# Borders between the stages of a two-layer decoder trunk rebuilt: order of the rows, of the expansion's products and of the contraction's sums

## The chip, the cores and the metric

The kernel runs on one core of a Trainium2 chip. The metric is device time in microseconds (us), the median of several executions. The engines are PE (matrix products), DVE (vector operations), ACT (activations, copies, casts), POOL (GpSimd) and SP, which here only issues DMAs. Each engine works through its own list of instructions in order; semaphores tie the lists together.

## What is computed

Two decoder layers over 1024 tokens of 1024 features, all in float32. Per layer, with gains left out:

```python
h = h + rmsnorm(mixer(rmsnorm(h)))        # layer 0: attention, layer 1: RG-LRU
u = rmsnorm(h)
f = square(relu(u @ w_up)) @ w_down       # 1024 -> 4096 -> 1024
h = h + rmsnorm(f)
h = h + rmsnorm(p @ w_proj) * sigmoid(h @ w_gate)
```

## The kernel before

**Precision.** Each float32 operand is split into a high and a low part (`split`: a cast on ACT, L115, and a subtraction on DVE, L116; names end in h and l), and each product runs as three matmuls, `mm3` (L147 to L149: high x high, high x low, low x high).

**The MLP** is done by Strassen's scheme in Winograd's form: seven products of half-size blocks in place of eight. Their operands are A11, A12, A22 (blocks of the weights) and S1 to S4 (sums of such blocks) on one side and B11, B21, B22, T1 to T4 (blocks and sums of the input, split once and kept in `comb`) on the other. "First half" and "second half" are the two halves of the tokens.

**The stages of a layer.** (1) The mixer. (2) `mix_out`: the output projection, row block by row block (eight of 128 tokens). Per row: 24 matmuls of 512 columns, a sum with the partial result `pt` (L954, two of 512 columns), a root mean square (square and sum on ACT L165, scale and power on POOL L167 and L170), a scaling with the gain on DVE (L174), the residual add on POOL (L888), the store of the row to `hD`, a second norm of the same kind, eight 128x128 transposes (L916) and the combinations of the blocks on DVE (`combine`, L934 to L941). Rows of the second half need those of the first (`held`), and the rows go in pairs, 4, 5, 0, 1, 6, 7, 2, 3 in layer 0. (3) `mlp_up`, the expansion: eight quads of 512 hidden features, each with seven products of 24 matmuls into pairs of PSUM banks, their sums, relu and square, and seven tiles of 512 KB that SP stores to DRAM (`hid`): already the block sums that the contraction needs. The order of the products is A11, A12, S2, S3, S1, A22, S4, with quads 0 and 1 starting together. (4) `mlp_down`, the contraction: four chunks of two quads, seven products of 48 matmuls, in the order A22, S1, S3, A11, S2, A12, S4. Each step loads two hidden tiles (`hraw`), splits them, and adds its result to its own accumulator (X and M tiles). In the last chunk 14 closing adds on DVE join the accumulators (L1109). (5) The gate: eight rows normed (`post`, once more with L888 on POOL), transposed (L183), multiplied with `ple_w_gate`.

**What sets the order.** The program is written stage by stage; a scheduler then fixes each engine's list before the run. `bufs` says how many buffers a name has, and a tile can't be written before the last reader of its buffer is done. `wAh` and `wAl`, the split weights, have three buffers each.

## Time and profile before

| | us |
|---|---|
| median of 3 runs | 2719.72 (2712.79 to 2722.66) |
| the profiled execution | 2716.89 |
| its span | 2715.1 |
| PE busy | 2515.9 (93%), mean granted clock 0.961 |
| DVE busy | 1685.8 (62%) |
| ACT busy | 1224.6 (45%) |
| POOL busy | 327.7 (12%) |

The stages of layer 0 end at about 652 (attention), 742 (output rows, norms and the first matmuls of the expansion), 1057.7 (expansion), 1378 (contraction), 1409 us (its norms); those of layer 1 lie 1212 us later. A view by stretch gives, for each engine, the busy time and the number of instructions in it, and the clock that was granted to PE. PE busy includes matmuls at a low clock, which take longer.

### The profile page before, as it was taken

How to read it: one execution, taken by the hardware profiler on the slowest of the kernel's cores; microseconds unless marked ns; L12 is line 12 of the kernel's file. 1: busy time of each engine (PE TensorE's matmuls, PEld its weight loads, DVE VectorE, ACT ScalarE, POOL GpSimd, SP SyncE). 2: the span in 40 equal slices, each digit the busy share in tenths (PEclk: the TensorE clock that was granted, in tenths of full speed). 3: DMA queues.
4: the chain of work that ended last, by engine and by line, in shares of the span. 5: the costliest groups of instructions: out<-in, count | busy, mean ns of one | idle time of the engine just before them, and what ended most of it. 6: DMA issues, size and time to landing. Idle time of an engine off the chain costs nothing. (4 is left out here: it accounts for less than half of the span.)

```text
span 2715.1 us, 31386 instructions
## 1 busy us (share of the span) xinstructions
PE 2515.9 (93%) x11681; PEld 2063.2 (76%) x11681; DVE 1685.8 (62%) x2094; ACT 1224.6 (45%) x1779; POOL 327.7 (12%) x398
## 2 busy tenths in 40 slices
PE   8899999988599999999969999998699999999969
PEld 7687888776478887877758788877578887877757
DVE  5565665765756656577774555654755665677862
ACT  4454555654434444433332366563443445433331
POOL 1312223313300000000050000002300000000050
PEclk9899999999799999999979999999799999999989
DMA  5747553435334447444353322245344446444253
GB/s 158 199 139 189 157 147 104 137 120 187 132 132 155 148 141 255 155 152 137 107 192 118 132 90 62 74 151 194 109 142 153 155 147 237 150 155 148 93 194 101
DMA packets 220893, 396.95 MB, mean 146 GB/s; under 512 B 16691, under 2 KB 118172, under 8 KB 220740
## 3 DMA queue, kind: packets, MB, share of 16 engines
q1 hardware_dynamic: 220740, 394.95, 44.9%
q8 instruction: 92, 1.51, 0.2%
q14 instruction: 61, 0.50, 0.1%
HBM read 273.63 MB, written 121.26 MB: 145 GB/s over the span
## 5 line engine op out<-in xcount | busy, mean ns | idle before, releaser
L148 PE MATMUL sc<-wAl,hh 128*128 128x512 f32 x896 | 356.2, 398 | 11.8 <-DVE wAl L116 11.8
L149 PE MATMUL sc<-wAh,hl 128*128 128x512 f32 x896 | 351.5, 393 | 0.0
L147 PE MATMUL sc<-wAh,hh 128*128 128x512 f32 x896 | 333.6, 396 | 12.9 <-ACT hh L115 12.9
L167 POOL TENSOR_SCALAR ms<-ss 128x1 f32<-128x1 f32 x112 | 49.5, 442 | 1877.2 <-ACT r L165 1598.4
L115 ACT CAST hh<-hraw 128x1024 fp32r<-128x1024 f32 x112 | 117.4, 1048 | 300.4 <-PE sc L148 294.5
L115 ACT CAST wAh<-S 128x1024 fp32r<-128x1024 f32 x128 | 134.2, 1048 | 198.1 <-PE sc L148 170.6
L148 PEld LDWEIGHTS sc<-wAl,hh 128*128 128x128 f32 x896 | 169.2, 189 | 59.6 <-DVE wAl L116 22.6
L116 DVE TENSOR_TENSOR hl<-hraw,hh 128x1024 fp32r<-128x1024 f32 x112 | 136.5, 1221 | 123.8 <-ACT hh L115 123.8
L147 PE MATMUL sc<-uh,wAh 128*128 128x512 f32 x512 | 201.9, 398 | 10.0 <-ACT wAh L115 10.0
L147 PEld LDWEIGHTS sc<-wAh,hh 128*128 128x128 f32 x896 | 169.2, 189 | 52.6 <-ACT hh L115 13.7
L149 PE MATMUL sc<-uh,wAl 128*128 128x512 f32 x512 | 205.9, 402 | 1.6 <-DVE wAl L116 1.6
L148 PE MATMUL sc<-ul,wAh 128*128 128x512 f32 x512 | 204.9, 400 | 0.0
L149 PEld LDWEIGHTS sc<-wAh,hl 128*128 128x128 f32 x896 | 168.7, 188 | 37.9
L116 DVE TENSOR_TENSOR wAl<-wraw,wAh 128x1024 fp32r<-128x1024 f32 (+1 forms) x100 | 129.7, 1298 | 71.9 <-ACT wAh L115 71.6
L116 DVE TENSOR_TENSOR wAl<-S,wAh 128x1024 fp32r<-128x1024 f32 x128 | 155.8, 1217 | 27.6 <-ACT wAh L115 27.6
L115 ACT CAST wAh<-wraw 128x1024 fp32r<-128x1024 f32 (+1 forms) x100 | 104.7, 1047 | 134.2 <-PE sc L148 53.6
L147 PE MATMUL sc<-xh,wAh 128*128 128x512 f32 x384 | 150.5, 392 | 1.8 <-ACT wAh L115 1.8
L149 PE MATMUL sc<-xh,wAl 128*128 128x512 f32 x384 | 152.1, 397 | 0.0
L148 PE MATMUL sc<-xl,wAh 128*128 128x512 f32 x384 | 151.9, 396 | 0.0
L402 DVE CUSTOM_DVE_ANT_0 sn<-sc,bias 128x128 f32<-128x128 f32 (+7 forms) x128 | 94.4, 754 | 67.0 <-PE tp L419 31.4
L147 PE MATMUL mm<-uh,wAh 128*128 128x512 f32 x312 | 127.7, 409 | 7.6 <-ACT st L342 6.6
L149 PE MATMUL mm<-uh,wAl 128*128 128x512 f32 x312 | 126.3, 405 | 0.0
(394 smaller groups left out, 6087.3 us busy)
## 6 DMA issues: line engine op xcount, KB each, us to landing
hraw<-hid SPq DMA_DIRECT2D x112, 512.0 KB
hid<-t SPq DMA_DIRECT2D x48, 512.0 KB
wq<-in_mlp_w_up_dram SPq DMA_DIRECT2D x44, 512.0 KB
wq<-in_mlp_w_down_dram SPq DMA_DIRECT2D x42, 512.0 KB
hD<-row SPq DMA_DIRECT2D x32, 512.0 KB
hid<-row SPq DMA_DIRECT2D x32, 512.0 KB
hid<-c SPq DMA_DIRECT2D x32, 512.0 KB
row<-hD SPq DMA_DIRECT2D x24, 512.0 KB
```

The lines of the kernel that those rows point to most:

```text
L115: nc.scalar.copy(out=dst_h, in_=src)
L116: nc.vector.tensor_tensor(out=dst_l, in0=src, in1=f32(dst_h), op=ALU.subtract)
L147: nc.tensor.matmul(dst, lh, rh, start=start, stop=False, skip_group_check=onto)
L148: nc.tensor.matmul(dst, lh, rl, start=False, stop=False, skip_group_check=onto)
L149: nc.tensor.matmul(dst, ll, rh, start=False, stop=stop, skip_group_check=onto)
L167: nc.gpsimd.tensor_scalar(out=ms, in0=ss, scalar1=1.0 / n, scalar2=eps, op0=ALU.mult, op1=ALU.add)
L402: nc.vector.tensor_tensor_reduce(out=sn[:, :w], in0=sps[:, :w], in1=bias, scale=-1.0, scalar=BIG, op0=ALU.add, op1=ALU.min, accum_out=nm)
```

## The change

- `mix_out`: the rows of the first half come first, 4, 5, 6, 7, 0, 1, 2, 3 in layer 0 and 0 to 7 in layer 1, and the attention's last units follow that order. A row's 24 matmuls go to one pair of banks with one load of the partial result. The norm's bias is added on ACT (`rms_row`), only the power stays on POOL, and the residual add is a fused scaling on DVE. The first half's transposed blocks are stored to DRAM (`uD`) and loaded again for the second half. Six products of the expansion, A11 and A12 of quads 0 to 2, are set among the rows by a list (`plan`); their weights use `wC` tiles and the usual buffers.
- `mlp_up`: the products come as A11, A12, S2, S1, S3, A22, S4. In the quads that were not begun early A11, S2, S3, A22 add up in one pair of banks, copied out in between, and S1, S4 in another. The hidden tiles of quads 0 and 1 are split on the spot (through `t`, three buffers) and stored as high and low tiles by POOL's queue (`hidS`).
- `first_step`: the contraction's first hidden tiles and weights are loaded and split before the expansion's last results.
- `mlp_down`: the order is A11, A12, S2, S3, A22, S1, S4, summed in PSUM; the 14 closing adds are gone. The first half of the rows is complete behind A22, two products before the end. The chunk of quads 0 and 1 comes last and loads its split tiles by POOL's queue, without splitting.
- The gate's norms use `rms_row` and DVE too; its products are as before.

Matmuls and transposes are the same in number. DVE's list goes from 2082 to 2057 rows, ACT's from 1541 to 1629, POOL's from 403 to 427, SP's from 985 to 951.

```diff
...
+    FACTOR = {"A11": B11, "A12": B21, "S2": T2, "S1": T1, "S3": T3, "A22": T4, "S4": B22}
+    NLEAD = 3
...
+    def rms_row(small, junk, src):
+
+        ss = small.tile([P, 1], F32, name="ss", bufs=4)
+        nc.scalar.activation(out=junk, in_=src, func=AF.Square, scale=1.0 / 32.0, accum_out=ss)
+        ms = small.tile([P, 1], F32, name="ms", bufs=4)
+        nc.scalar.activation(out=ms, in_=ss, func=AF.Identity, bias=eps1)
+        rs = small.tile([P, 1], F32, name="rs", bufs=4)
+        nc.gpsimd.tensor_tensor(out=rs, in0=ms, in1=nhalf, op=ALU.pow)
+        return rs
...
-            scale_gain(a, a, rs, g)
-            nc.gpsimd.tensor_tensor(out=h, in0=h, in1=a, op=ALU.add)
+            rs = rms_row(small, junk, a)
+            vec(ag, a, g, ALU.mult)
+            nc.vector.scalar_tensor_tensor(out=h, in0=ag, scalar=rs, in1=h, op0=ALU.mult, op1=ALU.add)
             return h
...
+                plan = [(out_row, 0), (out_row, 1), (combine, 0), (out_row, 2), (combine, 1), (out_row, 3),
+                        (combine, 2), (out_row, 4), (combine, 3), (out_row, 5), None, (combine, 4),
+                        (out_row, 6), None, (combine, 5), (out_row, 7), None, (combine, 6), None, None, None,
+                        (combine, 7)]
+                for step in plan:
+                    if step is None:
+                        leads.pop(0)()
+                    else:
+                        step[0](order[step[1]])
                 del wslots[3:]
...
+            def first():
+                a = st["A"] = pair_bank()
+                self.up_product(a, direct("A11", 0), "A11", True, True)
+                self.lead[q] = m1 = self.c.take()
+                nc.scalar.copy(out=m1[1], in_=a)
+
+            def second():
+                self.up_product(st["A"], direct("A12", 1), "A12", False, True)
+                c11 = row_tile()
+                self.squared(c11, st["A"])
+                nc.sync.dma_start(out=self.hidD[B11][q], in_=c11)
...
                     def keep(i, t):
-                        nc.sync.dma_start(out=hidD[i][q], in_=t)
...
+                        if q >= 2:
+                            nc.sync.dma_start(out=self.hidD[i][q], in_=t)
+                            return
+                        h, l = (hp.tile([P, D], F32R, name="t", bufs=3) for _ in range(2))
+                        split(h, l, t)
+                        for d, s in zip(self.hidS[i, q], (h, l)):
+                            nc.gpsimd.dma_start(out=d, in_=s)
...
+                    product(b, "S2", led)
+                    u2n, u2 = self.c.take()
+                    u3 = row_tile()
+                    if led:
+                        vec(u2, b, m1, ALU.add)
+                    else:
+                        nc.scalar.copy(out=u2, in_=b)
+                    c = pair_bank()
+                    product(c, "S1", True)
+                    product(b, "S3", False)
+                    if led:
+                        vec(u3, b, m1, ALU.add)
+                    else:
+                        nc.scalar.copy(out=u3, in_=b)
+                    vec(u3, c, u3, ALU.add)
...
+                    product(b, "A22", False)
...
+                    product(c, "S4", False)
+                    vec(u2, c, u2, ALU.add)
+                    c12 = u2
+                    self.squared(c12)
+                    if q == quads - 1:
+                        self.first_step()
...
+                if (i, q) in self.hidS:
+                    for d, s in zip((hh, hl_), self.hidS[i, q]):
+                        nc.gpsimd.dma_start(out=d, in_=s)
...
+        def first_step(self):
+            self.begin(0)
+            h, l = (t.rearrange("p (n a) c -> p n (a c)", n=2) for t in self.comb[B11])
+            self.ops0 = self.step("A11", [(h[:, n, :], l[:, n, :]) for n in range(2)])
...
-                        if c == last and name == "S4":
-                            for jj in range(2):
-                                h = home(jj)
-                                add(m6[jj], m6[jj], m1[jj])
...
+                for jj, b in product("A11", 0, True):
+                    onto((0, 0), jj, b, True)
+                for jj, b in product("A12", 1, True):
+                    onto((0, 0), jj, b)
+                for jj, b in product("S2", 0, False):
+                    temp("u2", jj, b)
+                for jj, b in product("S3", 0, False):
+                    temp("u3", jj, b)
+                for jj, b in product("A22", 0, False):
+                    onto((0, 1), jj, b, True)
+                yield c
+                for jj, b in product("S1", 2, True):
...
+                for jj, b in product("S4", 2, False):
...
-    m.mix_out(attn_w_out[0], (0, 2), lambda tb: x[0, tb * P:(tb + 1) * P, :], parts[0], (4, 5, 0, 1, 6, 7, 2, 3))
+    m.mix_out(attn_w_out[0], (0, 2), lambda tb: x[0, tb * P:(tb + 1) * P, :], parts[0], (4, 5, 6, 7, 0, 1, 2, 3))
```

**Where the lists change.** The names are tiles; `L116 ... wAl<-wq,wAh` (L118 in the new numbering) makes the low part of a weight, `S` are weight sums, `xl` and `ul` low parts of the combined input.

DVE in layer 0, from the last row's combination to the first products of the expansion, before:

```order
L116 TENSOR_TENSOR xl1_7482<-a_8091,xh1_7481 128x4x128
L116 TENSOR_TENSOR xl2_7484<-s_8028,xh2_7483 128x4x128
L116 TENSOR_TENSOR wAl_8179<-wq_8176,wAh_8178 128x1024
L116 TENSOR_TENSOR wAl_8211<-wq_8208,wAh_8210 128x1024
L116 TENSOR_TENSOR wAl_8246<-wraw_8243,wAh_8245 128x1024
L982 TENSOR_TENSOR S_8310<-wq_8311,wraw_8313 128x1024
L982 TENSOR_TENSOR S_8316<-S_8310,wq_8176 128x1024
L982 TENSOR_TENSOR S_8348<-wq_8176,wq_8311 128x1024
```

and after:

```order
L118 TENSOR_TENSOR ul01_130<-tp_8354,uh01_129 128x4x128
L118 TENSOR_TENSOR xl1_7572<-u_8362,xh1_7571 128x4x128
L118 TENSOR_TENSOR xl2_7574<-row_8359,xh2_7573 128x4x128
L878 TENSOR_TENSOR S_8390<-wq_8392,wq_8394 128x1024
L878 TENSOR_TENSOR S_8391<-S_8390,wraw_8397 128x1024
L878 TENSOR_TENSOR wraw_8397<-wraw_8397,wq_8392 128x1024
L878 TENSOR_TENSOR wq_8544<-wq_8544,S_8391 128x1024
L878 TENSOR_TENSOR S_8608<-wq_8610,wraw_8612 128x1024
L118 TENSOR_TENSOR wAl_8401<-S_8391,wAh_8400 128x1024
```

Before, the first three low weights stand right behind the last combination. Now five weight sums stand between it and the first low weight, that of S2.

ACT in the middle of a quad of the expansion, layer 0, before (`c` and `row` are the results' tiles, `sc` PSUM):

```order
L115 CAST wAh_9021<-S_9019 128x1024
L1038 COPY c_8944<-sc_8913 128x1024
L115 CAST wAh_9052<-S_8947 128x1024
L115 CAST wAh_9081<-wraw_8950 128x1024
L1031 ACTIVATE row_9015<-sc_8913 128x1024
L1032 ACTIVATE row_9015<-row_9015 128x1024
L115 CAST wAh_9113<-S_8953 128x1024
```

and after:

```order
L117 CAST wAh_9178<-wq_9080 128x1024
L1142 COPY c0_9112<-sc_9008 128x1024
L117 CAST wAh_9211<-wq_9044 128x1024
L117 CAST wAh_9257<-wq_9255 128x1024
L1149 COPY row_9113<-sc_9008 128x1024
L1068 ACTIVATE row_9113<-row_9113 128x1024
```

The copy of `row_9113`, the result behind S3, stands behind the casts of two later products' weights; before, `c_8944` was the only copy of the quad, and the first relu of `row_9015` read its bank directly.

PE at the place of `COPY row_9113` (S3 ends with the third row, A22 begins with the last):

```order
L149 MATMUL sc_9008<-xh1_7571,wAh_9145 128x512
L150 MATMUL sc_9008<-xl1_7572,wAh_9145 128x512
L151 MATMUL sc_9008<-xh1_7571,wAl_9146 128x512
L149 MATMUL sc_9252<-uh10_135,wAh_9257 128x512
L150 MATMUL sc_9252<-ul10_136,wAh_9257 128x512
L149 MATMUL sc_9008<-xh2_7573,wAh_9178 128x512
```

S3 and A22 stand next to each other on the bank `sc_9008`, with two matmuls of the next quad's A11 (weight `wAh_9257`) between them.

DVE behind the contraction's last product in layer 0, before (`X` are the result rows):

```order
L174 SCALAR_TENSOR_TENSOR X00_10149<-X00_10149,rs_12332,gain_12323 128x1024
L1109 TENSOR_TENSOR X01_10150<-X01_10150,M_10154 128x2x512
L174 SCALAR_TENSOR_TENSOR X00_10149<-X00_10149,rs_12344,gain_12323 128x1024
L1109 TENSOR_TENSOR X10_10151<-sc_12252,X10_10151 128x2x512
L116 TENSOR_TENSOR wAl_12817<-wraw_12815,wAh_12816 128x1024
L1109 TENSOR_TENSOR X11_10152<-sc_12278,X11_10152 128x2x512
L116 TENSOR_TENSOR wAl_12823<-wraw_12821,wAh_12822 128x1024
L174 SCALAR_TENSOR_TENSOR X01_10150<-X01_10150,rs_12370,gain_12323 128x1024
L174 SCALAR_TENSOR_TENSOR X01_10150<-X01_10150,rs_12396,gain_12323 128x1024
L174 SCALAR_TENSOR_TENSOR X10_10151<-X10_10151,rs_12422,gain_12323 128x1024
L174 SCALAR_TENSOR_TENSOR X10_10151<-X10_10151,rs_12448,gain_12323 128x1024
L116 TENSOR_TENSOR ul10_12315<-tp_12349,uh10_12314 128x4x128
```

and after:

```order
L878 TENSOR_TENSOR X11_10264<-sc_12236,X11_10264 128x2x512
L118 TENSOR_TENSOR wAl_12844<-wraw_12842,wAh_12843 128x1024
L878 TENSOR_TENSOR X11_10264<-X11_10264,c2_12352 128x1024 x2
L118 TENSOR_TENSOR ul10_12344<-tp_12380,uh10_12343 128x4x128
L118 TENSOR_TENSOR ul11_12342<-av_12387,uh11_12341 128x4x128
L918 SCALAR_TENSOR_TENSOR row_12444<-X10_10263,rs_12450,row_12444 128x1024
L118 TENSOR_TENSOR ul10_12344<-tp_12405,uh10_12343 128x4x128
L118 TENSOR_TENSOR ul11_12342<-mm_12412,uh11_12341 128x4x128
L118 TENSOR_TENSOR ul10_12344<-tp_12430,uh10_12343 128x4x128
L118 TENSOR_TENSOR ul11_12342<-av_12437,uh11_12341 128x4x128
L918 SCALAR_TENSOR_TENSOR row_12469<-X10_10263,rs_12475,row_12469 128x1024
L918 SCALAR_TENSOR_TENSOR row_12494<-X11_10264,rs_12500,row_12494 128x1024
```

The scalings of the last four rows come in both lists among the splits of transposed rows (`ul`); the closing adds of `M` to `X` are gone, and each row has a product with the gain (`c2`) and a fused scaling and add (L918).

## Rows read from the trace of the kernel before

**Rows 1.** Table by stretch, layer 0: length, busy us of each engine, granted clock, DMA.

```profile
core 0: us, PE busy (x) PEld busy (x) DVE busy (x) ACT busy (x) POOL busy (x), PEclk, DMA share, GB/s
652.00:732.20 80.20, 50.58 (x224) 39.72 (x222) 57.90 (x75) 39.06 (x74) 39.62 (x40) 0.82 0.47 156
732.20:742.00 9.80, 8.97 (x23) 6.61 (x24) 7.76 (x8) 1.88 (x2) 0.00 (x0) 0.58 0.07 13
742.00:1051.00 309.00, 307.20 (x1322) 248.82 (x1320) 183.19 (x155) 129.90 (x126) 0.00 (x0) 1.00 0.45 153
1051.00:1057.70 6.70, 0.14 (x1) 0.00 (x0) 4.72 (x4) 4.11 (x4) 0.00 (x0) 0.75 0.99 390
1057.70:1345.00 287.30, 286.58 (x1226) 230.08 (x1227) 199.51 (x172) 117.08 (x121) 0.00 (x0) 0.99 0.46 154
1345.00:1378.00 33.00, 27.95 (x119) 21.80 (x117) 31.63 (x28) 9.47 (x12) 7.61 (x5) 1.00 0.30 88
1378.00:1408.00 30.00, 11.66 (x51) 9.40 (x51) 27.59 (x23) 14.71 (x26) 27.59 (x19) 0.57 0.70 247
```

**Rows 2.** The same table, layer 1.

```profile
1866.00:1944.00 78.00, 49.35 (x215) 38.99 (x213) 61.05 (x74) 39.34 (x74) 39.23 (x40) 0.79 0.48 162
...
2590.00:2620.00 30.00, 11.72 (x50) 9.51 (x51) 27.49 (x23) 14.70 (x26) 27.49 (x19) 0.62 0.67 235
```

**Rows 3.** Waits of PE, 652 to 742 us: us in total, times, longest.

```profile
PE tp L916 <- DVE a L174: 24.6, 8, 7.3
PE sc L147 <- ACT wAh L115: 4.1, 1, 4.1
```

**Rows 4.** Waits of PE, 742 to 1345 us.

```profile
PE sc L147 <- ACT hh L115: 6.6, 1, 6.6
PE sc L147 <- ACT wAh L115: 1.8, 2, 0.9
```

**Rows 5.** Waits of PE, 1345 to 1410 us.

```profile
PE tp L183 <- POOL row L888: 10.1, 4, 6.1
PE av L183 <- DVE X L1109: 5.1, 1, 5.1
```

**Rows 6.** Instructions by line, POOL, 652 to 742 us: count, busy, mean ns, idle before.

```profile
L888 POOL TENSOR_TENSOR row<-row,a 128x1024 f32<-128x1024 f32 x8 | 19.1, 2388 | 13.7 <-DVE a L174 13.7
L170 POOL TENSOR_TENSOR rs<-ms,nhalf 128x1 f32<-128x1 f32 x16 | 13.6, 849 | 1.3
```

**Rows 7.** Instructions by line, DVE, 652 to 742 us.

```profile
L174 DVE SCALAR_TENSOR_TENSOR a<-a,rs,gain 128x1024 f32<-128x1024 f32 x8 | 10.3, 1282 | 3.3 <-POOL rs L170 3.3
...
L934 DVE TENSOR_TENSOR a<-tp,s 128x512 f32<-128x512 f32 x4 | 2.7, 685 | 1.3 <-PE tp L916 1.3
...
L982 DVE TENSOR_TENSOR S<-wq 128x1024 f32<-128x1024 f32 x1 | 1.2, 1220 | 0.0
```

**Rows 8.** Instructions by line, ACT, 742 to 1345 us.

```profile
L115 ACT CAST wAh<-S 128x1024 fp32r<-128x1024 f32 x62 | 65.0, 1048 | 89.0 <-PE sc L148 85.3 <-issue 3.7
...
L1147 ACT COPY M<-sc 128x1024 f32<-128x1024 f32 x6 | 6.1, 1010 | 11.9 <-PE sc L149 11.9
```

**Rows 9.** From the page, DMA queues: packets, MB, share of 16 engines.

```profile
q1 hardware_dynamic: 220740, 394.95, 44.9%
```

**Rows 10.** Instructions by line, DVE, 1345 to 1410 us.

```profile
L174 DVE SCALAR_TENSOR_TENSOR X<-X,rs,gain 128x1024 f32<-128x1024 f32 x8 | 14.2, 1800 | 2.4 <-POOL rs L170 2.4
L1109 DVE TENSOR_TENSOR X<-X,M 128x1024 f32<-128x1024 f32 x8 | 9.6, 1216 | 0.0
```

**Rows 11.** PE in order of time, the last matmul before the norms, the first behind.

```profile
1377.65 0.40 PE L149 MATMUL sc<-wAh,hl 128*128 128x512 f32 x1
...
1409.34 0.49 PE L147 MATMUL tp<-wq,uh 128*128 128x512 f32 x1
```

**Rows 12.** Instructions by line, POOL, 620 to 660 us.

```profile
L170 POOL TENSOR_TENSOR rs<-ms,nhalf 128x1 f32<-128x1 f32 x10 | 5.5, 550 | 0.8
```

**Rows 13.** Instructions by line, POOL, 1345 to 1410 us.

```profile
L170 POOL TENSOR_TENSOR rs<-ms,nhalf 128x1 f32<-128x1 f32 x8 | 9.2, 1157 | 0.4
```

More of the change, by code (lines that the diff above doesn't have):

```diff
@@ L74, in tile_hybrid_trunk @@
     nc.vector.memset(one1, 1.0)
+    eps1 = const.tile([P, 1], F32, name="eps1")
+    nc.vector.memset(eps1, EPS)
     def row_tile():
@@ new lines, in step @@
+        def step(self, name, hl=None):
+            i = FACTOR[name]
+            ops = []
+            for n, q in enumerate(self.chunk):
+                hh, hl_ = hl[n] if hl else (self.dn.tile([P, D], F32R, name=f"h{x}", bufs=4) for x in "hl")
+                if (i, q) in self.hidS:
+                    for d, s in zip((hh, hl_), self.hidS[i, q]):
+                        nc.gpsimd.dma_start(out=d, in_=s)
+                else:
+                    rn, raw = self.c.take()
+                    nc.sync.dma_start(out=raw, in_=self.hidD[i][q])
+                    split(hh, hl_, raw)
+                    self.c.give(rn)
+                wh, wl = self.weights(self.sums[n], name, self.As[n],
+                                      lambda s: self.mw.tile([P, D], F32, name="S", bufs=4))
+                ops += [[t[:, p * 512:(p + 1) * 512] for t in (hh, hl_, wh, wl)] for p in range(2)]
+            return ops
@@ L1178, in mlp_and_ple @@
                     drain(1)
-                g2 = None if last else self.gain(mp, ln_mix_pre[layer + 1:layer + 2, :])
                 for nh in range(2):
```

471 lines of the change are left out of this document (254 added, 217 removed).

## The prediction

> **What bounds the kernel now.** I read the table by stretch first. TensorE (PE) works nearly without a hole inside the two MLP stages: 307.2 of 309.0 us in the expansion, 286.6 of 287.3 in the contraction, clock 1.00 and 0.99 [rows 1]. The expansion's row gives 307.20 / 1322 = 0.232 us per 512-wide matmul, so a product of 24 is 5.6 us and one of the contraction (48) 11.1 us. What is lost lies at the borders. I count a border's loss as its length minus PE busy times granted clock, so that slow matmuls count too. Layer 0: output rows and norms 80.2 - 50.58 x 0.82 = 38.7, and the stretch behind them 9.8 - 8.97 x 0.58 = 4.6, together 43.3 us; expansion to contraction 6.6; contraction's end 33.0 - 27.95 = 5.1; its norms 30.0 - 11.66 x 0.57 = 23.4. That is 78 us. Layer 1 repeats it, with 39.0 and 22.7 at the two large ones [rows 2]. Some 155 us of the 2715 can be had at most.
>
> Then the waits of PE at each border. At the first it waits for VectorE (DVE): eight transposes for a scaled row, 24.6 us, then 4.1 for a weight's cast on ScalarE (ACT) [rows 3]. At the second, one wait of 6.6 us for the cast of a hidden tile [rows 4] while the DMAs run at 390 GB/s, share 0.99 [rows 1]. At the third it is GpSimd's (POOL's) row add, 10.1 us, and DVE's last sum, 5.1 [rows 5]. So the borders are chains over DVE, ACT and POOL, and what counts is how long these chains are afterwards. Everything below is per layer, gain positive.
>
> **1. Output rows and norms, with six products set among them (-1 us).** Removed: the POOL add of 2.39 us per row [rows 6]; a row now has, on DVE, a sum and a gain product (1.22 each, the price of a 1024-wide tensor op [rows 7]) and two fused scalings at 1.28 [rows 7]. POOL keeps the power, 0.85 us here [rows 6]. Six products move from the expansion into this stretch, 6 x 5.6 = 33.4 us of PE work. So PE has 8 rows x 24 x 0.232 = 44.5, eight rows' transposes about 7 and 33.4: 85 us. DVE, by the order shown ahead, has before the last row's transposes 16 ops at 1.22, 16 at 1.28, some 35 of 512 columns at 0.69 [rows 7] and 5 low weights at 1.22: 70 us. Behind the transposes stand nine combination ops at 0.69, five weight sums and only then the low weight of S2, 6 x 1.22: 13.5 us. The sums belong to S1, S3 and S4 and to quad 1, yet S2's low weight is queued behind all of them, and no product is left on PE to cover it. In the old order the same tail is there, with three products' weights that are ready. DVE was busy 65.7 of the 90 us before (57.90 + 7.76 [rows 1]); with 83.5 us of ops and a similar chain of norms I place S2 at 100 us. PE loses 15 there, 4 more at the low clock that follows such a hole (0.58 in the 10 us behind it [rows 1]), and 3 because the attention's last transposes no longer mix with the rows.
>
> The first quads then pay. Quads 0 and 1 split their hidden tiles on the spot: 7 more splits each on ACT (1.05 [rows 8]) and DVE (1.22), through three `t` buffers. DVE has 71 ops, 86.6 us, from S2's low weight to quad 3; PE has 15 products in that time, 83. The sum u2 of quad 1 stands behind 13 such ops of quad 0, and S3 reuses its bank: 10 us. The `t` buffers add 4, quad 2's A22 some 5, the rest 3. Together 15 + 4 + 3 + 22 = 44 against 43.3 before: -1. Bounds: +10 if the norms' chain is fully overlapped (S2 at 90), -12 if the `t` buffers come back one us later per tile (14 / 3 = 4.7 us for each of two quads).
>
> **2. Quads 3 to 7 (-8 us).** S3 and A22 now follow each other on one PSUM bank, and S3 must be copied out between them. ACT's order has the cast of the next quad's first weight ahead of that copy; its slot is freed by S3's last matmul but one. So 1.05 (cast) + 1.01 (copy) [rows 8] + some 0.25 for two handovers, less three matmuls, 0.7, that PE has meanwhile: 1.6 us, five times, 8. Before, S1 stood between S3 and A22 and hardly anything waited (1.8 us in all for two casts [rows 4]). Ends: 4, where the cast is free earlier, and 9.5.
>
> **3. Expansion to contraction (+7 us).** The first step's hidden tiles and weights are loaded and split inside the last quad, and PE goes on 45 matmuls behind the last result. The 6.6 us wait goes [rows 4]; its cover is the last quad, whose DMA share is 0.45 as a mean [rows 1]. 6 to 8.
>
> **4. The contraction's chains (-3) and its last chunk (-1.5).** Sums now wait in PSUM. S3 and A22 run at two 24-matmul passes on a bank each, and a third weight slot comes free only at the end of the product before: about 0.9 us (one late cast [rows 4]), one or two in each of four chunks. I take 3; ends 1 and 9. The last chunk reads 28 tiles of 512 KB that were split already, from POOL's queue: 14.7 MB in 77 us, with the weights 243 GB/s against 154 before [rows 1]. The trace has shown 390 GB/s [rows 1], so there is room; what is not shown is POOL's queue, since nearly all of before's bytes, 394.95 of 396.95 MB, go through SP's [rows 9]. I take 1.5, nearest to that row; ends 0 and 15 (a tile late by 1 us in half of the 28).
>
> **5. Contraction's end to gate (+14 us).** The 14 closing sums on DVE go (1.22 each [rows 10]: 17 us, partly beside PE), and with POOL's add gone the scaling, 1.80 beside POOL [rows 10], should be 1.28 again [rows 7]. Four rows are normed under the last two products. But the last four remain, and PE's order still has seven rows' transposes ahead of the first gate matmul, as before. DVE has behind the last product, by the order shown, a sum, two weights, two gain products, six splits and three scalings, some 5 x 1.22 + 6 x 0.69 + 3 x 1.28 = 14.1, and the seventh row's transposes and the handovers make it 17.6 us. Before, the last product began its last matmul at 1377.65 and the gate its first at 1409.34 [rows 11], 31.5 us apart. 31.5 - 17.6 = 13.9; of the 5.1 lost ahead of it 1.5 is saved, and as much goes to the low clock. 14, between 8 and 18.
>
> **Sum.** -1 - 8 + 7 - 3 - 1.5 + 14 = +7.5 per layer, 15 in all. The profiled execution took 2716.89 us (span 2715.1); 2716.9 - 15 = 2701.9. The median of the runs, 2719.72, lies 2.8 above it: **2705**. All ends kind: 10 - 4 + 8 - 1 + 0 + 18 = 31 per layer, 2658; all unkind: -12 - 9.5 + 6 - 9 - 15 + 8 = -31.5, 2783.
>
> **Rivals.** (a) *The borders are really filled.* If ACT and POOL are so much ahead that DVE does the sums under the last three set-in products, S2 isn't late (15 + 4 us) and quad 1 doesn't inherit the backlog (some 6): 25 per layer, of which I leave 5 to waits that then show: 2705 - 2 x 20 = 2665. For it: DVE idles a quarter of the stretch now. Against: the tail of 13.5 us hangs on the last transposes, whatever is ahead.
>
> (b) *Slower: POOL's queue holds the `t` buffers.* At the mean 153 GB/s of the expansion [rows 1] 512 KB take 3.4 us. The walk bears a store that holds its buffer up to 4.2 us; from there each us costs 4.7 per quad, since DVE waits for a buffer with the weights of PE queued behind. POOL's instructions are stretched when DVE is busy: its power takes 0.55 us in a quiet stretch [rows 12], 0.85 among the first norms [rows 6], 1.16 among the last [rows 13], a factor of 2.1. If the making of descriptors suffers like that, a store takes 3.4 x 2.1 = 7.1 us, 2.9 too long: 14 per quad, four quads in two layers, 2705 + 56 = 2761. Against: DVE was busy 183.2 of the expansion's 309 us [rows 1], so POOL would often find it idle. The Trainium skill, SBUF — State Buffer, section "SBUF: two separate sides", says that transfers issued on GpSimd's queue get their descriptors from GpSimd, that it is locked out of a shared port while VectorE runs some of its operations, and that the same transfer from another queue is not held up. By that rule (b) would hold if the splits here were such operations; the power's 0.55 to 1.16 us agrees that the two engines hinder each other, and no row shows a transfer. The same skill, DMA: Bandwidth & Descriptors, section "Anatomy of one DMA — SWDGE (gpsimd) path", fits 2.0 us + bytes / 436e3 us, an estimate of 3.2 us per store, which would leave the sum as it is.
>
> (c) *It doesn't do what it says at the ends.* Seven rows' transposes still stand ahead of the gate; if the norm chain of the last rows is as long as now (POOL's power 1.16 us, waits between), the gate border gives 5 instead of 14: 2705 + 18 = 2723.
>
> **Chances.** The forecast, 2688 to 2722, 0.42; (a) 0.22; (b) 0.19; (c) 0.17. A measurement here tells a change from none at about 0.5%, that is 2706 and 2733. Of the forecast's 0.42 I give 0.24 to below 2706; (a) is all faster: 0.46 faster. Same: 0.18 and 0.14 of (c), 0.32. Slower: (b) and the rest of (c), 0.22. The range goes from the kind sum, 2658, to 2757, which leaves out the upper half of (b) and the edge of (a).
>
> **What would show it.** Right: PE waits of 13 to 15 us for a low weight before the first S2, with clock 0.5 to 0.6 behind it; waits near 1 us twice before each A22 of quads 3 to 7, for a cast and for a copy; no wait at the start of the contraction; 17 to 18 us from the last product to the gate. Wrong: `t` tiles for which DVE or ACT waits on a DMA for more than 4 us (then b); a first S2 right behind the last transposes (a); a gate more than 25 us after the last product (c); or steady quads that lose much more or less than 1.6 us each.

## The result and the profile after

The changed kernel takes 2755.65 us (median of four runs, 2754.74 to 2760.15), the kernel before beside it 2719.07 us (2712.79 to 2722.66): ratio 1.014, interval 1.0118 to 1.0162. It is 36.6 us slower. 2705 was forecast, 15 faster: the sign is wrong, though the time lies just inside the range that was given as a whole, 2658 to 2757. The profiled execution took 2754.74 us, its span is 2752.9, 37.8 longer than before's 2715.1.

I begin with the table by stretch of layer 0, the columns as in [rows 1]: length, busy us of each engine, granted clock, DMA share, GB/s.

```profile
652.00:736.60 84.60, 76.17 (x350) 61.85 (x348) 62.47 (x70) 50.01 (x92) 11.09 (x15) 0.94 0.58 211
736.60:748.10 11.50, 0.01 (x1) 0.00 (x0) 9.00 (x12) 5.34 (x10) 0.00 (x0) 0.70 0.68 228
748.10:830.00 81.90, 58.43 (x229) 45.14 (x230) 48.00 (x43) 28.52 (x28) 8.22 (x15) 0.83 0.51 167
830.00:1067.20 237.20, 230.57 (x976) 182.14 (x975) 132.80 (x114) 112.54 (x110) 6.91 (x13) 1.00 0.51 178
1067.20:1084.60 17.40, 10.53 (x47) 8.19 (x45) 9.60 (x9) 8.04 (x8) 0.00 (x0) 0.94 0.69 252
1084.60:1360.00 275.40, 271.29 (x1139) 214.00 (x1140) 185.81 (x160) 103.50 (x106) 10.60 (x20) 0.99 0.51 171
1360.00:1399.00 39.00, 37.47 (x159) 29.32 (x158) 29.44 (x26) 16.16 (x27) 9.53 (x14) 1.00 0.72 243
1399.00:1418.20 19.20, 10.63 (x58) 9.35 (x56) 17.35 (x21) 10.79 (x21) 1.42 (x3) 0.70 0.68 229
```

PE is now well filled among the rows (76.17 of 84.6 us, clock 0.94; before 50.58 of 80.2, 0.82 [rows 1]) and the way from the last product to the gate is shorter (19.2 us in the last row; 31.3 before, by [rows 11]). The new loss is in the third row: 58.43 of 81.9 us, clock 0.83, where before PE worked nearly without a hole (307.20 of 309.00 us [rows 1]). PE's larger waits (us in all, times, longest; [rows 3, 4] answer to them) come in three groups: layer 0 from 652 to 820 us, that is the rows and the first quads; layer 0 from 820 to 1110, past the border of the contraction; and layer 1 in the stretch of its rows and first quads (two of its lines).

```profile
PE sc L149 <- DVE c L878: 20.2, 1, 20.2
PE sc L149 <- ACT wAh L117: 12.5, 2, 11.5
PE tp L975 <- DVE a L176: 8.4, 1, 8.4
...
PE sc L149 <- ACT wAh L117: 13.2, 8, 6.9
PE sc L149 <- ACT row L1149: 0.9, 5, 0.2
...
PE sc L149 <- DVE c L878: 15.7, 1, 15.7
PE tp L975 <- DVE a L176: 15.0, 2, 8.5
```

So the costliest single wait is for `c`, the sum u2 of quad 1, 20.2 us and in layer 1 15.7; 11.5 us are the first S2's weight; 8.4 us, in layer 1 15.0 in two waits, are for a scaled row among the rows; 6.9 us, the longest of the second group, are the border to the contraction, as long as before (6.6).

From marks in both traces I get the balance, gain positive. The marks are the attention's last scaled block (`oq`), the first S2 (before: the first product of the expansion, with the 33.4 us of the six products added), the last matmul of the expansion, the last of the contraction and the gate's first.

| | layer 0 | layer 1 | forecast per layer |
|---|---|---|---|
| attention up to its last scaled block | +10.3 | (in the row below) | 0 |
| rows to first S2, less 33.4 us for the six products | +7.2 | -0.4 | +21 |
| expansion from S2 on | -33.6 | -33.0 | -22 -8 |
| border and contraction | -5.0 | -4.7 | +7 -4.5 |
| last product to gate | +12.3 | +12.8 | +14 |
| behind the gate | | -3.6 | 0 |

The sum, -8.8 - 28.9 = -37.7, is the span's 37.8. The attention's 10.3 us need not be the work of the change: among 14 kernels (the changed one and 13 made from it below) whose engines' lists are the same up to there, this block ends between 636.6 us, in the changed kernel's own trace, and 647.1; in the kernel before it ends at 646.9. There is one trace of each kernel, so whether this spread belongs to the kernel or to the single execution is open.

### The profile page after: what moved, and what is told of

Its sections match the earlier page's. It is cut to its first block, busy times and chain, and to the rows that moved or that the text cites. A ratio compares the mean times of both kernels' runs of the same rounds, so it can differ in the third digit from the quotient of the medians.

```text
span 2752.9 us, 31458 instructions
## 1 busy us (share of the span) xinstructions
PE 2531.9 (92%) x11681; PEld 2051.0 (75%) x11681; DVE 1656.4 (60%) x2075; ACT 1266.9 (46%) x1867; POOL 274.4 (10%) x422
## 5 line engine op out<-in xcount | busy, mean ns | idle before, releaser
L150 PE MATMUL sc<-wAl,hh 128*128 128x512 f32 x864 | 346.6, 401 | 7.5 <-DVE wAl L118 7.4
L149 PE MATMUL sc<-uh,wAh 128*128 128x512 f32 x464 | 185.6, 400 | 9.0 <-ACT wAh L117 9.0
L150 PE MATMUL sc<-ul,wAh 128*128 128x512 f32 x464 | 183.8, 396 | 0.0
L151 PE MATMUL sc<-uh,wAl 128*128 128x512 f32 x464 | 183.1, 395 | 0.0
L117 ACT CAST hh<-c 128x1024 fp32r<-128x1024 f32 x80 | 83.6, 1048 | 203.7 <-PE sc L150 190.4
L118 DVE TENSOR_TENSOR wAl<-wraw,wAh 128x1024 fp32r<-128x1024 f32 (+1 forms) x94 | 120.4, 1282 | 94.4 <-ACT wAh L117 94.0
L118 DVE TENSOR_TENSOR wAl<-wq,wAh 128x1024 fp32r<-128x1024 f32 x80 | 97.6, 1220 | 96.7 <-ACT wAh L117 96.6
L118 DVE TENSOR_TENSOR hl<-c,hh 128x1024 fp32r<-128x1024 f32 x80 | 97.5, 1220 | 95.3 <-ACT hh L117 95.3
L117 ACT CAST wAh<-wq 128x1024 fp32r<-128x1024 f32 x80 | 83.8, 1047 | 137.9 <-PE sc L150 132.1
L149 PEld LDWEIGHTS sc<-xh,wAh 128*128 128x128 f32 x384 | 74.5, 194 | 92.1 <-issue 36.7
L150 PE MATMUL mm<-ul,wAh 128*128 128x512 f32 x312 | 124.5, 399 | 0.0
```

The costliest lines, as they stand in the source:

```text
L117: nc.scalar.copy(out=dst_h, in_=src)
L118: nc.vector.tensor_tensor(out=dst_l, in0=src, in1=f32(dst_h), op=ALU.subtract)
L149: nc.tensor.matmul(dst, lh, rh, start=start, stop=False, skip_group_check=onto)
L150: nc.tensor.matmul(dst, lh, rl, start=False, stop=False, skip_group_check=onto)
L151: nc.tensor.matmul(dst, ll, rh, start=False, stop=stop, skip_group_check=onto)
```

## The experiments

Each time stands against the kernel before on the same chip. Where two changed kernels differ by less than 4 us or so, I draw nothing from it. Since the attention alone can shift a trace by 10 us, I also compare stretches that begin behind it.

**What makes u2 late?** DVE in order of time, quad 0's last splits and then the sum (start, length, what; in brackets the idle time before and who ended it):

```profile
804.57 1.23 DVE L118 TENSOR_TENSOR t<-row,t 128x1024 fp32r<-128x1024 f32 x1 [2.31 <-DMA hidh<-t]
810.58 1.23 DVE L118 TENSOR_TENSOR t<-c,t 128x1024 fp32r<-128x1024 f32 x1 [4.79 <-DMA hidh<-t]
811.84 1.22 DVE L878 TENSOR_TENSOR c<-sc,c 128x1024 f32<-128x1024 f32 x1
```

The last row is u2: it has no idle time of its own, it stands at the end of DVE's list of that time. In PE's hole DVE is busy 12.90 us (table in the last section) and waits 2.31 and 4.79 for a `t` buffer to be stored. S3 begins on u2's bank at 813.21, after 20.15 us. DVE's waits from 745 to 815 us, grouped:

```profile
DVE t L118 <- DMA hidh<-t: 10.6, 4, 4.8
DVE S L878 <- DMA wq<-in_mlp_w_up_dram: 8.4, 3, 3.7
DVE wq L878 <- DMA wq<-in_mlp_w_up_dram: 3.7, 1, 3.7
```

Stores take 10.6 us of it and weight loads 12.1. Three theories: the splitting itself and its stores (A); their place in POOL's queue (the rival (b) of the prediction); the order of the products, which leaves only S1, 24 matmuls or 5.6 us, between quad 1's S2 and S3 to cover a late DVE.

*No early split*: quads 0 and 1 store their hidden tiles whole, the last chunk splits them as the others do.

```diff
-                          for i in range(7) for q in range(2)}
+                          for i in range(7) for q in range(0)}
...
-                        if q >= 2:
+                        if True:
...
-                        if q < 2:
-                            keep(B11, c11)
```

> The hidden tiles of quads 0 and 1 are stored whole by SP again and split in the last chunk of the contraction like all others; nothing else changes. Theory A (the splits' three t buffers hold DVE, and with it the sum u2 for which PE waits 20.2 us in layer 0 and 15.7 in layer 1): this wait falls under 3 us, the low clock behind it goes too, some 20 us per layer, 2755.7 - 40 = 2715 (2706 to 2724). Theory B (DVE's plain backlog of weight sums and evictions, the t buffers only add to it): the wait stays above 10 us, 2740 to 2750. If the tiles that are split early saved something in the last chunk, the contraction gets longer by that; I expect under 3 us per layer.

Measured 2750.47 us (2746.17 to 2754.03), ratio 1.0113 (1.0089 to 1.0138). The wait for `c`:

```profile
PE sc L149 <- DVE c L878: 7.2, 1, 7.2
```

20.2 became 7.2, and layer 0 from S2 to the border is 12 us shorter. But the contraction from its second product on grew from 314.6 to 321.9 us: in its last chunk DVE must split again, and PE waits 3.9 us for one weight. So A is a part of u2's wait, but the splitting moved from one end to the other is worth little: the two ends nearly cancel.

*Stores on SP's queue* instead of POOL's, with three buffers as before. The DRAM tiles are declared F32 for it, with the same bytes.

```diff
-            self.hidS = {(i, q): [dram.tile([P, D], F32R, name=f"hid{x}{layer}_{i}_{q}") for x in "hl"]
+            self.hidS = {(i, q): [dram.tile([P, D], F32, name=f"hid{x}{layer}_{i}_{q}") for x in "hl"]
...
-                            nc.gpsimd.dma_start(out=d, in_=s)
+                            nc.sync.dma_start(out=d, in_=f32(s))
```

> The split tiles are stored by SP's queue in place of POOL's; the splits, the three t buffers and the loads stay. Theory A1 (POOL's making of descriptors is what keeps a t buffer): landing falls clearly below the 3.2 and 3.5 us of now, the wait of 20.2 us to under 8, time 2725 to 2735. Theory A2 (three buffers for 14 tiles per quad and transfers that share the DMA engines with weight loads: any queue is too slow): landing stays at 3 us or more, the wait changes by less than 5 us, time 2745 to 2760.

Measured 2749.03, 1.0109 (1.0076 to 1.0142).

```profile
PE sc L149 <- DVE c L878: 16.3, 1, 16.3
```

16.3 of 20.2 us are left, and DVE still waits 7.2 us for stores instead of 10.6: POOL's queue is a small part of the wait, and what is left goes with the splits, their three buffers and DVE's list.

*S4 ahead of A22*, so that S1 is followed by S3 on the one bank, S4 on the other, and then A22. S1's result is read first for it, so that S4 can be added on S1's bank; nothing else is changed.

```diff
-                    product(b, "S3", False)
                     if led:
-                        vec(u3, b, m1, ALU.add)
+                        vec(u3, c, m1, ALU.add)
                     else:
-                        nc.scalar.copy(out=u3, in_=b)
-                    vec(u3, c, u3, ALU.add)
+                        nc.scalar.copy(out=u3, in_=c)
+                    product(b, "S3", False)
+                    vec(u3, b, u3, ALU.add)
...
+                    product(c, "S4", False)
+                    vec(u2, c, u2, ALU.add)
+                    c12 = u2
+                    self.squared(c12)
                     product(b, "A22", False)
...
-                    product(c, "S4", False)
-                    vec(u2, c, u2, ALU.add)
-                    c12 = u2
-                    self.squared(c12)
```

> The changed kernel with S4 ahead of A22 in the expansion, and S1's result copied out first, so that no two neighbouring products share a bank. Theory A (S3 and A22 next to each other cost 1.84 us per quad, the cast and the copy on ACT): quads 3 to 7 go from 40.8 us to 39.0, quads 0 to 2 gain a little, 2755.7 - 20 = 2736 (2731 to 2742). Theory B (another engine is as late there): less than 5 us of difference.

Measured 2705.85 (2702.83 to 2710.76), 0.9957 (0.9947 to 0.9968): 50 us less than the changed kernel, more than twice what I had expected. PE's waits from 735 to 1060 us, whole:

```profile
PE sc L149 <- ACT wAh L117: 14.5, 3, 11.3
PE sc L151 <- DVE wAl L118: 2.1, 2, 1.4
PE sc L149 <- DVE row L878: 2.1, 1, 2.1
PE sc L149 <- DVE c L878: 0.8, 1, 0.8
```

The wait for `c` is gone with all splits and POOL's stores still in place, and so are the five waits for `row` and the small ones for casts. In PE's list 74 matmuls (17.2 us) now stand between the last one of quad 1's S2 and the first of its S3, instead of 24 (5.6 us): S1 and S4 of quad 1, S2 of quad 2, which needs no bank of theirs, and two more. To see which quads pay, the new order was put into quads 0 to 2 alone, and then into quads 3 to 7 alone (the code above under a condition on `led`).

> S4 ahead of A22 (and S1 copied out first) in quads 0 to 2 alone, quads 3 to 7 as in the changed kernel. Theory A (in the early quads PE has only one product, S1, between S2 and S3, and S3 waits for the sum u2 that stands on DVE behind quad 0's chain; with S4 free of S3 the list has four products in that place): the waits of 20.2 and 15.7 us fall under 4, the time by 36 to 44, 2716 (2710 to 2722). Theory B (the neighbours on one bank in quads 3 to 7 are the larger part of the 50 us): less than 20 us.

> S4 ahead of A22 in quads 3 to 7 alone, quads 0 to 2 as in the changed kernel. Theory A: these five quads go from 40.8 us to 39.0, nine per layer, and the waits for u2 stay at 20 and 16: 2755.7 - 18 = 2738 (2732 to 2744). Theory B: 2725 or less.

Measured 2729.37, 1.003 (1.0016 to 1.0043) for the first three, and 2735.11, 1.0053 (1.0035 to 1.0071) for the others. The former is 26 us below the changed kernel, less than the 36 to 44 expected; the latter is as expected. The former's wait for `c` and the latter's:

```profile
PE sc L149 <- DVE c L878: 0.9, 1, 0.9
```

```profile
PE sc L149 <- DVE c L878: 17.6, 1, 17.6
```

From S2 to the wait at the border, layer 0, the changed kernel takes 329.5 us, the first of these 315.0, the second 320.4, both together 306.4. So -14.5 and -9.1 add up to the -23.1 of both: the order is worth 14.5 us in quads 0 to 2, where it covers u2, and 1.8 us in each of quads 3 to 7.

**The steady quads.** The forecast said cast and copy one behind the other, 1.6 us. The same place one period apart (PE, in order of time):

```profile
891.41 0.49 PE L149 MATMUL sc<-uh,wAh 128*128 128x512 f32 x1 [0.90 <-ACT wAh L117]
```

```profile
932.23 0.50 PE L149 MATMUL sc<-uh,wAh 128*128 128x512 f32 x1 [0.91 <-ACT wAh L117]
```

40.82 us for 168 matmuls, 38.98 at 0.232 each: 1.84 lost. *The copy on DVE* should shorten it if ACT's order, cast ahead of copy, is what costs:

```diff
-                        nc.scalar.copy(out=u3, in_=b)
+                        nc.vector.tensor_copy(out=u3, in_=b)
```

> The changed kernel with the copy of S3's result in quads 3 to 7 on DVE in place of ACT; the order of the products stays. Theory A (of the 1.84 us per quad one half is the cast on ACT, the other the copy queued behind it): the copy runs beside the cast, 0.9 us less per quad, 2755.7 - 9 = 2747 (2743 to 2751), and the waits for u2 (20.2 and 15.7 us) stay within 2 us. That would leave 40 of the 50 us of the run with S4 ahead of A22 to u2's wait. Theory B (the copies on ACT are what delays u2 as well): below 2735.

Measured 2752.58, 1.0127 (1.0107 to 1.0147). The period is 40.37: a quarter of the loss goes. The casts' 0.9 us stay, as does u2's wait, 20.0. So the rest isn't the copy's place on ACT; it goes whole when another bank's product stands between the two, in the order above.

**The six products among the rows.** *All behind the rows:*

```diff
-                        (combine, 2), (out_row, 4), (combine, 3), (out_row, 5), None, (combine, 4),
-                        (out_row, 6), None, (combine, 5), (out_row, 7), None, (combine, 6), None, None, None,
-                        (combine, 7)]
+                        (combine, 2), (out_row, 4), (combine, 3), (out_row, 5), (combine, 4),
+                        (out_row, 6), (combine, 5), (out_row, 7), (combine, 6),
+                        (combine, 7)] + [None] * 6
```

> The six products that are set among the norms come behind the last row instead. View 1 (they fill holes of the norms): without them the holes come back, some 25 us per layer, 2755.7 + 50 = 2806. View 2 (behind the rows they cover DVE's tail of sums, 13.5 us, so that most is not lost): 5 to 10 us per layer, 2766 to 2776.

Measured 2747.07, 1.0101 (1.0074 to 1.0128). Both expectations, 2766 and more, were wrong: it is 8.6 us faster than with the products among the rows. The wait of 8.4 us for a scaled row is gone, replaced by small ones of 2.6 and less, and the one ahead of S2 is 6.1 instead of 11.5:

```profile
PE sc L149 <- ACT wAh L117: 13.4, 9, 6.1
```

The 8.4 us of the changed kernel do not lie behind a set-in product, but ahead of the first one (PE in order of time):

```profile
684.85 1.94 PE L975 MATMUL tp<-ident,a 128*128 128x128 f32 x8 [8.43 <-DVE a L176]
686.61 0.79 PE L149 MATMUL sc<-uh,wCh 128*128 128x512 f32 x1
```

In PE's list there, the fourth row's transposes follow the third row's at once, and the seventh row's matmuls come only behind them, mixed with the first product. With the products behind the rows, some 32 matmuls of rows stand between these two groups of transposes, and the wait is gone (in layer 1 15.0 us become 3.1). So the six products pushed later rows' matmuls out of the places where these cover the rows' own chain on DVE and ACT; and behind the rows the products cover a part of DVE's tail ahead of S2. That the shorter time is not the attention's spread is shown by the stretch from the attention's last scaled block to S2: 111.1 to 112.6 us in the nine kernels with the products among the rows, 105.3 to 107.8 in the five that have them behind.

**The border to the contraction.** *No first step* inside the expansion:

```diff
-                    if q == quads - 1:
-                        self.first_step()
...
-                if c:
-                    self.begin(c)
+                self.begin(c)
...
-                    ops = self.ops0 if c == 0 and name == "A11" else self.step(name)
+                    ops = self.step(name)
```

> The contraction's first step is no longer loaded and split inside the last quad. Prediction's view (first step hides the border's wait of 6.6 us): 7 us more per layer, 2755.7 + 14 = 2770. Other view (the wait of 6.9 us that is now seen after the first 45 matmuls is the same wait for weights whose buffers come free only with the expansion's end, moved by one product): PE's waits there are 10 us or less in sum and the time is 2753 to 2764.

Measured 2766.51, 1.0173 (1.0143 to 1.0203): 10.9 slower than the changed kernel, so the first step is worth 5.5 us per layer (2.6 and 6.6 by the stretch from S2 to the contraction's last matmul). Yet in the changed kernel the border waits 6.9 us all the same. The first product does start at once, but it lasts only 10.4 us, and then A12's weight `wx` is missing. SP's queue (start, length, transfers):

```profile
1074.72 0.70 SPq L915 DMA_DIRECT2D row<-hD  x1
1075.61 1.22 SPq L1115 DMA_DIRECT2D hid<-row  x1
1076.92 1.09 SPq L1048 DMA_DIRECT2D wx<-in_mlp_w_down_dram  x2
1078.10 1.19 SPq L1048 DMA_DIRECT2D wy<-in_mlp_w_down_dram  x1
```

`wx` is issued at 1076.92, behind the last quad's stores, whose products ended at 1067; and the DMAs are full in the wait and behind it (table by stretch, columns as above):

```profile
1077.70:1084.60 6.90, 0.05 (x1) 0.06 (x1) 1.45 (x3) 3.41 (x4) 0.00 (x0) 0.84 1.03 406
1084.60:1101.00 16.40, 16.36 (x60) 12.66 (x61) 16.24 (x15) 7.05 (x7) 0.00 (x0) 0.86 1.04 405
```

If SP's list is what makes it late, *`wx` and `wy` on POOL's queue* should help:

```diff
-                    nc.sync.dma_start(out=t.rearrange("p (a n) -> p a n", a=src.shape[1]), in_=src)
+                    q_ = nc.gpsimd if name in ("wx", "wy") and self.chunk == (2, 3) else nc.sync
+                    q_.dma_start(out=t.rearrange("p (a n) -> p a n", a=src.shape[1]), in_=src)
```

> The changed kernel with one edit: in the contraction's first chunk the weights that need new buffers (wx, wy) are loaded by POOL's queue. Theory A (they are late because SP issues them behind the last quad's stores, at 1076.9, while their buffers are free since the last result at 1067): the wait of 6.9 us at the contraction's second step falls under 3, 2755.7 - 9 = 2747 (2743 to 2751). Theory B (the DMA engines are full there, 405 GB/s for 24 us, whoever issues): less than 4 us of difference.

Measured 2778.65, 1.0223 (1.02 to 1.0246), 23 us slower. PE then waits behind 1087 us, for weights' casts, 8.4 us in three waits up to 1110, and the DMAs are as full:

```profile
1087.00:1102.00 15.00, 7.45 (x18) 4.53 (x17) 5.27 (x5) 5.91 (x6) 1.42 (x2) 0.73 1.03 401
```

POOL issues `wx` at 1047.6, long before its use, so SP's list did hold it back; and of the three waits the one at the border is 3.9 us instead of 6.9. But a wait for `wy`'s buffer at the head of POOL's list lasts 39 us, to 1088, and holds what stands behind it. From S2 to the contraction's last matmul the layers are 12.5 and 13.2 us longer than in the changed kernel; the attention's 9.5 us more in this trace come on top. That the stage's start is bound by the DMAs' rate is likely, and not shown: a lighter load there was not tried.

**The norms and the gate.** *The kernel before, with the residual add on DVE* (gain product and fused scaling) and nothing else:

```diff
-            scale_gain(a, a, rs, g)
-            nc.gpsimd.tensor_tensor(out=h, in0=h, in1=a, op=ALU.add)
+            nc.vector.tensor_tensor(out=a, in0=a, in1=g, op=ALU.mult)
+            nc.vector.scalar_tensor_tensor(out=h, in0=a, scalar=rs, in1=h, op0=ALU.mult, op1=ALU.add)
```

> The kernel before with one part of the change alone: the residual add of the norms (rows of the out projection and rows behind the contraction) leaves POOL; DVE does a gain product and a fused scale-and-add instead. Theory A (POOL's add of 2.4 to 2.6 us is in the chain PE waits for, 10.1 us at the gate, and slows DVE's scaling from 1.28 to 1.80): the gate border gets 6 to 9 us shorter per layer, the first border 2 to 4, 2720 - 20 = 2700 (2694 to 2706). Theory B (DVE is last there anyway, and gets 1.2 us more work per row): 2715 to 2722.

Measured 2706.58 (2704.12 to 2714.74), 0.9964 (0.9952 to 0.9976). Two lines alone give 11 us. DVE's scaling at the gate, 1800 ns before [rows 10]:

```profile
L888 DVE SCALAR_TENSOR_TENSOR row<-X,rs,row 128x1024 f32<-128x1024 f32 x8 | 10.1, 1278 | 1.7 <-issue 1.7
```

The gate comes 26.2 us behind the last product instead of 31.3; the add of 2.39 us on POOL [rows 6] both made DVE slower and stood in the chain. *The changed contraction and gate alone*, on the kernel before, without first step or early split (`mlp_down`, `step`, `add_norm` and `rms_row` as in the change):

```diff
-            rows = self.mlp_down(hidD, macc)
+            for _ in self.mlp_down(macc):
+                pass
...
+            rows = self.rows
...
-                    h = self.post(mp, tb, g1, rows[tb], hD[tb])
+                    a = rows[tb]
+                    h = self.add_norm(tb, g1, a, a, hD[tb], (j1, j2)[n % 2], mp)
```

> The kernel before up to the end of the expansion, with the changed contraction and gate (order A11, A12, S2, S3, A22, S1, S4 summed in PSUM, chunk of quads 0 and 1 last, norms on ACT and DVE), but without first step and without tiles split early. The gate border is 14 us shorter per layer, as in the changed kernel. Theory A (the contraction pays for it: waits of 0.42 us at each second weight, about 5 per layer, the first step's 5.5, and 7 in the last chunk, whose splits stand among the norms): 14 - 17.5 = -3 per layer, 2720 + 7 = 2727 (2718 to 2735). Theory B (the waits in the contraction of the changed kernel come from what the expansion leaves over): 2720 - 20 = 2700.

Measured 2717.87 (2712.84 to 2726.17), 0.9993 (0.998 to 1.0006). The waits around the gate are now small ones (PE, 1345 to 1410 us):

```profile
PE tp L185 <- DVE ul L118: 4.6, 2, 2.7
PE sc L150 <- DVE wAl L118: 4.1, 2, 3.9
PE tp L149 <- DVE ul L118: 1.9, 1, 1.9
```

but what the gate gains the contraction gives back. From the last product's last matmul to the gate's first it is 1385.29 to 1405.06, 19.8 us instead of 31.7 [rows 11]; from the contraction's first matmul to its last it is 335.0 us, and 319.9 before. One wait of 3.9 us in the last chunk, with the low clock behind it (0.85 in the next 11.7 us), and one of 3.3 for a copy out of PSUM are in that; the border ahead gains 5.5 (1.1 us of wait instead of 6.6 [rows 4]). So the contraction's new order, with its chains in PSUM, gains nothing by itself here: it costs what the gate gains.

**Putting the findings together.** S4 first with the six products behind the rows (both edits above), in four forms, each by the edits shown: without the early split; with it and `wx`, `wy` on POOL's queue; with those loads on POOL's queue and no early split; and with the early split and SP's loads.

> The changed kernel with three parts undone or mended: hidden tiles of quads 0 and 1 stored whole, the six products behind the last row, S4 ahead of A22. If the three add up (5, 8.6 and 20 us): 2755.7 - 34 = 2722 (2714 to 2730). If the early quads' wait for u2 is one cause that all three touch, they don't add up: 2732 to 2742.

> S4 ahead of A22, the six products behind the last row, and the weights of the contraction's second step loaded by POOL's queue; the tiles of quads 0 and 1 are still split early. If the gains of the single runs add up: 2705.9 - 8.6 - 8 = 2689 (2683 to 2697). If the second step's weights are late for another reason than their place in SP's queue, 2694 to 2700.

> As the run with S4 ahead, products behind the rows and weights on POOL's queue, but with the tiles of quads 0 and 1 stored whole. If splitting early is worth its 7 us per layer in the last chunk once PE no longer waits for u2: 10 to 14 us slower than that run. If it costs as much in the expansion as it saves in the contraction: within 4 us of it.

> S4 ahead of A22 in all quads and the six products behind the last row; the tiles are split early and all loads are on the changed kernel's queues. If what the place of the six products gave (8.6) adds to the order's 50: 2697 (2692 to 2702). If it was the same wait: 2704 to 2708. Beside the run that also stores whole tiles (2697.6) it tells what splitting early is worth: as fast, nothing; 8 us faster, its gain in the last chunk.

In this order 2697.57, 0.9926 (0.9897 to 0.9954); 2706.25, 0.9951 (0.9934 to 0.9968); 2705.64, 0.9956 (0.994 to 0.9972); and **2693.61** (2688.8 to 2693.9), 0.9895 (0.9874 to 0.9917). The last is faster than both kernels, 25.7 us below before, and within what was expected. The first had been put at 2722, with 20 us for the order where it gave 50; the second, put at 2689, missed by 17. What splitting early is worth once u2 isn't waited for stays unclear: the second and third differ by 0.6 us against it, the first and last by 4.0 for it. `wx` and `wy` on POOL's queue cost 8 to 13 us here too. Against S4 first alone (2705.85) the last gains 12.2 us by the place of the six products, so that place is worth 9 to 12 us in both orders. Its table by stretch:

```profile
660.00:744.50 84.50, 77.86 (x348) 61.55 (x346) 67.46 (x78) 52.10 (x97) 14.67 (x15) 0.96 0.61 216
744.50:830.00 85.50, 71.89 (x283) 55.56 (x283) 58.63 (x51) 35.16 (x34) 8.78 (x16) 0.92 0.61 204
830.00:1055.60 225.60, 225.59 (x967) 181.16 (x965) 130.78 (x112) 114.48 (x112) 6.41 (x12) 1.00 0.54 191
```

The steady quads have no hole left, 225.59 of 225.60 us, and the stretch of the first quads holds 71.89 us of PE work at clock 0.92, against 58.43 at 0.83 in the changed kernel. PE's longest wait from 735 to 1060 us is 6.1, for S2's weight.

## Why the prediction was wrong

**Term 1 failed, at two steps.** The first is "I place S2 at 100 us". DVE's tail was read rightly, 11.5 us of wait for S2's weight against 13 to 15 forecast; but the chain of the rows itself has waits for scaled rows, 8.4 us in layer 0 and 15.0 in layer 1, which the term had at nothing, and of +21 us 7 came in layer 0 and none in layer 1. Behind it stands that the six products were taken as free cover: set among the rows they move later rows' matmuls behind these waits, and set behind the rows they save 8.6 us. The second step is "the first quads then pay", 22 us. It came out as 24.4 (33.6 less 9.2 for the steady quads; 23.8 in layer 1) by the mechanism named, a bank that waits for u2; that the total is so near is partly luck, for this one wait took 20.2 us where I gave 10. I costed the wait and passed over its cause: the order S2, S1, S3 leaves one product as cover, and moving S4 takes the wait away. The term's unkind bound of -12 was too near: layer 0 has 7.2 - 24.4 = -17.2, layer 1 -24.2.

**Term 2 held**: 1.84 us in each of five quads against 1.6, 9.2 in all, inside 4 to 9.5, and PE waits where it was forecast, for a cast (0.9) and then for the copy (0.2). The copy on DVE shows that the copy's place on ACT is only a quarter of it.

**Term 3 failed**: +7 was 0. The first step has its worth, 5.5 us per layer by its removal, but I asked only whether the first product is ready, not what the second one needs. The wait went from the first hidden tile to the second product's weight, 6.9 us for 6.6.

**Term 4 held in size only**: 5.0 and 4.7 lost against 4.5 (that includes the border's change, nearly nothing). Its main part was to be late casts on ACT, one or two of 0.9 us in each chunk. There is one; the others wait for low parts on DVE, 4.0 us in all, and before it was 5.7 (PE, 1086 to 1401 us):

```profile
PE sc L150 <- DVE wAl L118: 4.0, 10, 1.5
PE sc L149 <- ACT wAh L117: 1.1, 1, 1.1
```

In all the waits behind the border are no longer than before, and the clock in the 25.5 us behind it is 0.91 against 0.93. Where most of the 5 us goes I did not find, so the near hit is luck in part. **Term 5 held**: 12.3 and 12.8 against 14, by the price seen with POOL's add gone, 1275 ns:

```profile
L918 DVE SCALAR_TENSOR_TENSOR row<-X,rs,row 128x1024 f32<-128x1024 f32 x6 | 7.6, 1275 | 1.8 <-DMA row<-hD 1.7
```

What is missing is the 3.6 us behind layer 1's gate; some 2 of them are the clock, 0.86 in the 14.7 us behind it, where before it was 1.00.

**The rivals.** (a) is out: S2 is late. (c) is out: the gate is 19 us behind the last product. (b) gave 2761, near what was measured, yet its cause is not the one found. It wanted stores stretched to 7.1 us in POOL's queue; they landed in 3.2 and 3.5 us (last column: median from issue to landing):

```profile
hidh<-t POOLq DMA_DIRECT2D x28, 512.0 KB, 3.2
hidl<-t POOLq DMA_DIRECT2D x28, 512.0 KB, 3.5
hh<-hidh POOLq DMA_DIRECT2D x28, 512.0 KB, 5.0
hl<-hidl POOLq DMA_DIRECT2D x28, 512.0 KB, 6.2
```

That median doesn't show each store; DVE's longest wait for one was 4.8 us. SP's queue took only 4 of the 20 us away, and with S4 first the wait is gone though the same stores stay in POOL's queue. The estimate from the Trainium skill, DMA: Bandwidth & Descriptors, section "Anatomy of one DMA — SWDGE (gpsimd) path", was 3.2 us for each: the stores agree, the loads of the same size, 5.0 and 6.2, do not.

So of the 31.5 us per layer between forecast (+7.5) and balance (-24.0 as the mean of the layers without the attention's 10.3), some 20 are term 1 (-1 against -17.2 and -24.2) and 7 are term 3. The chance of 0.22 for slower was too low, as I see it, for the same reason: each wait was given a size on its own, and none was seen to be able to double, as u2's did, when DVE's list and its stores were late together.

Three of the forecast's small sums don't come out of their own figures: [rows 11] gives 31.7 us, not 31.5; the unkind end of term 1 is -1 - 9.4 = -10.4, not -12; and one late cast of 0.9 us in each of four chunks is 3.6, not 3. None of them turns the sign.

Open: why the weights `wq` came late for DVE in the first quads (12.1 us, present in the kernel with no early split as well), and the attention's spread.

## What to carry over

When products are put on fewer PSUM banks, count for each bank how many matmuls stand between the product that fills it and the next one on it, and compare that with the backlog of the engine that must empty it, at its worst place and not in the steady state; a change of the order alone moved this kernel by 50 us. Work that is to fill a border belonged, in this kernel, where the chain ends, behind its last link, and not in its middle, where it took the place of the chain's own cover. When a first step is drawn ahead, look at the second step's loads too: in which queue they stand, behind which stores.

## What I had not expected of the hardware

- A hole of 20.2 us in PE's work has a granted clock of 0.57, and the 11.8 us behind it 0.87 (table by stretch):

```profile
793.00:813.20 20.20, 0.06 (x1) 0.02 (x1) 12.90 (x11) 6.02 (x6) 4.64 (x9) 0.57 0.90 300
813.20:825.00 11.80, 10.89 (x40) 8.45 (x41) 3.49 (x3) 2.07 (x2) 0.00 (x0) 0.87 0.12 44
```

Behind it 10.89 x 0.87 = 9.5 us of full-speed work were done in 11.8, so 2.3 us more than the hole itself; I had charged 4 for the first border.

- POOL's power takes 746 ns among the norms although POOL computes nothing else there now, 849 before [rows 6], 808 in the kernel before with only the add moved to DVE, and 550 in a quiet stretch [rows 12]; so POOL's own add explains only a part of what stretches it, and the rest wasn't tested:

```profile
L887 POOL TENSOR_TENSOR rs<-ms,nhalf 128x1 f32<-128x1 f32 x15 | 11.1, 746 | 64.4 <-ACT ms L885 63.1 <-DVE a L176 1.3
```

- 512 KB from POOL's queue land 3.2 to 3.5 us behind their issue as stores, and 5.0 to 6.2 as loads in the last chunk, where the DMAs moved 243 GB/s.
